# Contrast adjustment on one core: scaling and clip moved from ScalarE and VectorE to two whole-tile VectorE passes

## The chip, the cores and the metric

The kernel runs on one core of one Trainium2 chip. The metric is the device time of one execution in microseconds (us). The timed figure is longer than the span of the same execution in its profile (239.35 against 237.5 for the kernel before), so timed and traced numbers are kept apart below.

## The reference

```python
def reference(x, factor):                      # x: 16 x 3 x 512 x 512 float32, factor 1.5
    mean = np.mean(x, axis=(2, 3), keepdims=True)
    return np.clip(mean + factor * (x - mean), 0, 1).astype(np.float32)
```

The input is read once and an output of the same size is written once: 50.33 MB each way. An image must be summed before its first pixel can be written, so the work is load, sum, scale and clip, store.

## The kernel before

The 48 images are 12 tiles of 128 x 8192 float32 (4.19 MB each). A ring of six tile buffers lies in on-chip memory. SyncE issues the loads, ScalarE issues the stores. A tile is summed by two engines side by side (VectorE 4352 columns, ScalarE 3840), a matmul with a constant block matrix adds up the partitions of each image, and the result is a per-partition bias. Then ScalarE computes `relu(1.5 * x + bias)` in place, in two chunks, and VectorE takes the minimum with 1 behind it.

```python
BUFS = 6
CHUNKS = (5120, 3072)
SHORT = 2048
FIRST = (SHORT, 3072, 3072)
SUM = 4352
# ... (cut: pools, blockw, load)
    def compute(t):
        xt = ring[:, t % BUFS, :]
        sums = rpool.tile([P, 2], f32, name="sums")
        nc.vector.tensor_reduce(                                            # L78
            out=sums[:, 0:1], in_=xt[:, 0:SUM], axis=mybir.AxisListType.X, op=Alu.add
        )
        junk = jpool.tile([P, ROW - SUM], f32, name="junk")
        nc.scalar.activation(                                               # L82
            out=junk, in_=xt[:, SUM:ROW], func=Act.Copy, accum_out=sums[:, 1:2]
        )
        pbias = psum.tile([P, 1], f32, name="pbias")
        nc.tensor.matmul(pbias, blockw, sums[:, 1:2], start=True, stop=False)   # L86
        nc.tensor.matmul(pbias, blockw, sums[:, 0:1], start=False, stop=True)   # L87
        bias = bpool.tile([P, 1], f32, name="bias")
        nc.vector.tensor_copy(out=bias, in_=pbias)                          # L89
        c = 0
        for n in FIRST if t == 0 else CHUNKS:
            part = xt[:, c : c + n]
            nc.scalar.activation(out=part, in_=part, func=Act.Relu, bias=bias, scale=factor)  # L93
            nc.vector.tensor_scalar(out=part, in0=part, scalar1=1.0, scalar2=None, op0=Alu.min)  # L94
            # ... (cut: tile 0 stores its first 2048 columns early)
            c += n
        store(t, FIRST[0] if t == 0 else 0, ROW)                            # issued by ScalarE, L101
# ...
        load(0, c1=SHORT); load(0, c0=SHORT); load(1); load(2, n=2); load(4, n=2)
        for t in range(n_tiles):
            compute(t)
            if t + BUFS < n_tiles:
                load(t + BUFS)             # waits until the store of tile t has landed
```

## Time and profile before

| | kernel before |
|---|---|
| timed, median of the first 3 runs | 239.18 us (239.09 to 239.86) |
| span in the profile | 237.5 us |
| moved | 100.67 MB |
| VectorE busy, ScalarE busy | 111.9 us (47%), 131.1 us (55%) |
| rate from 100 to 200 us | 435 GB/s |

The page of the kernel before: busy time by engine, then the rows of VectorE, ScalarE and DMA over 40 equal slices of the span (a digit is tenths of the slice busy), the rate of each slice, and the chain of waits that ended last.

```profile
PE 14.0 (6%) x48; PEld 12.0 (5%) x48; DVE 111.9 (47%) x49; ACT 131.1 (55%) x50; POOL 0.9 (0%) x9
...
DVE  0073846161964343782928739173462733716000
ACT  2058678056679046769676796753680690593000
...
DMA  7999999999999999999999999999999999999996
GB/s 297 410 441 441 417 441 356 459 430 451 436 419 430 403 436 441 441 441 436 441 436 436 425 419 414 436 443 441 436 441 430 441 436 419 425 414 441 441 441 265
...
DMA 57%; DVE 19%; ACT 10%; another core or an unknown queue 3%; issue 1%; PE 1%; SPq 1%; ACTq 0%
```

Read the DMA row first: it is at 9 from the second slice to the last but one, while both compute engines have holes throughout. A single slice's rate scatters, so the rate is better read from a longer stretch. The view by stretches gives, for each, its length, the busy time of each engine, the clock, the DMA share and the rate:

```profile
100.00:200.00 100.00, 7.03 (x24) 6.00 (x24) 56.71 (x25) 64.82 (x24) 0.00 (x0) 1.00 1.01 435
```

The groups of instructions by shape give what one piece of work costs. After the count come total busy time, mean nanoseconds of one, and the engine's idle time before them.

```profile
L78 DVE TENSOR_REDUCE sums<-ring 128x1 f32<-128x4352 f32 x12 | 56.2, 4682 | 41.4 <-DMA ring<-in_x_dram 41.4
L93 ACT ACTIVATE ring<-ring,bias 128x5120 f32<-128x5120 f32 x11 | 50.2, 4562 | 19.9 <-DVE bias L89 11.0 <-issue 8.9
...
L94 DVE TENSOR_SCALAR ring<-ring 128x5120 f32<-128x5120 f32 x11 | 31.1, 2827 | 51.5 <-ACT ring L93 51.5
```

VectorE waits 41.4 us in total for loads: compute waits for data. The timeline shows the last tile, from its load's landing (202.79, the reduce's start) to its store's issue (217.53). The columns are start, duration, engine and instruction.

```profile
202.79 4.69 DVE L78 TENSOR_REDUCE sums<-ring 128x1 f32<-128x4352 f32 x1 [4.65 <-DMA ring<-in_x_dram]
...
208.16 0.16 DVE L89 COPY bias<-pbias 128x1 f32<-128x1 f32 x1 [0.68 <-PE pbias L87]
208.40 7.31 ACT L93 ACTIVATE ring<-ring,bias 128x5120 f32<-128x5120 f32 x2 [2.05 <-issue]
212.99 4.51 DVE L94 TENSOR_SCALAR ring<-ring 128x5120 f32<-128x5120 f32 x2 [4.68 <-ACT ring L93]
217.53 0.34 ACTq L101 DMA_DIRECT2D out_dram<-ring  x1
```

The chain of this tile is 217.53 - 202.79 = 14.74 us. The store lands at the span's end, 20 us after its issue.

### The profile page before, as it was taken

The numbers are of one execution on the slowest core, as the hardware profiler recorded it, in microseconds if no ns is written. First come the engines' busy times: TensorE is split into PE (matmuls) and PEld (weight loads), VectorE is DVE, ScalarE is ACT, GpSimd is POOL, SyncE is SP. The second block draws the span as 40 slices with busy tenths as digits, with TensorE's granted clock in tenths as the row PEclk, the third lists the DMA queues.
The fourth block names the chain that finished last, engine by engine and source line by source line (L and its number), as shares of the span: only waits on it lengthen the run. The fifth ranks groups of instructions, "written<-read, shape, count | busy, mean of one in ns | idle before, by whom it ended". The sixth has DMA issues, their size and how long they took to land.

```text
span 237.5 us, 307 instructions
## 1 busy us (share of the span) xinstructions
PE 14.0 (6%) x48; PEld 12.0 (5%) x48; DVE 111.9 (47%) x49; ACT 131.1 (55%) x50; POOL 0.9 (0%) x9
## 2 busy tenths in 40 slices
PE   0010010001010001010010100100100100100000
PEld 0010010001010001010010100100100100100000
DVE  0073846161964343782928739173462733716000
ACT  2058678056679046769676796753680690593000
POOL 1000000000000000000000000000000000000000
DMA  7999999999999999999999999999999999999996
GB/s 297 410 441 441 417 441 356 459 430 451 436 419 430 403 436 441 441 441 436 441 436 436 425 419 414 436 443 441 436 441 430 441 436 419 425 414 441 441 441 265
DMA packets 3713, 100.67 MB, mean 424 GB/s; under 512 B 384, under 2 KB 384, under 8 KB 384
## 3 DMA queue, kind: packets, MB, share of 16 engines
q1 hardware_dynamic: 1840, 50.33, 49.7%
q10 hardware_dynamic: 1872, 50.33, 49.1%
q14 instruction: 1, 0.01, 0.0%
HBM read 50.33 MB, written 50.33 MB: 424 GB/s over the span
## 4 chain that ended last, share of the span: by engine, by line
DMA 57%; DVE 19%; ACT 10%; another core or an unknown queue 3%; issue 1%; PE 1%; SPq 1%; ACTq 0%
DMA ring<-in_x_dram 40%; DMA out_dram<-ring 17%; ACT ring L93 10%; DVE ring L94 9%; DVE sums L78 9%; PE pbias L87 1%; SPq L73 1%; DVE bias L89 0%; ACTq L93 0%
## 5 line engine op out<-in xcount | busy, mean ns | idle before, releaser
L93 ACT ACTIVATE ring<-ring,bias 128x3072 f32<-128x3072 f32 (+2 forms) x25 | 87.9, 3564 | 22.1 <-DVE bias L89 13.2
L94 DVE TENSOR_SCALAR ring<-ring 128x3072 f32<-128x3072 f32 (+2 forms) x25 | 54.3, 2208 | 56.1 <-ACT ring L93 56.1
L78 DVE TENSOR_REDUCE sums<-ring 128x1 f32<-128x4352 f32 x12 | 56.2, 4682 | 41.4 <-DMA ring<-in_x_dram 41.4
L82 ACT ACTIVATE junk<-ring 128x3840 f32<-128x3840 f32 x12 | 40.8, 3402 | 61.8 <-DMA ring<-in_x_dram 48.5
L86 PE MATMUL pbias<-sums,blockw 128*128 128x1 f32 x24 | 7.0, 361 | 190.1 <-ACT junk L82 190.1
L86 PEld LDWEIGHTS pbias<-sums,blockw 128*128 128x128 f32 x24 | 6.0, 311 | 191.0 <-ACT junk L82 174.6
L87 PE MATMUL pbias<-sums,blockw 128*128 128x1 f32 x24 | 7.0, 362 | 3.9 <-DVE sums L78 3.4
L87 PEld LDWEIGHTS pbias<-sums,blockw 128*128 128x128 f32 x24 | 6.0, 311 | 5.0 <-DVE sums L78 5.0
L89 DVE COPY bias<-pbias 128x1 f32<-128x1 f32 x12 | 1.9, 158 | 8.1 <-PE pbias L87 8.1
L82 ACT ACTIVATION_READ_ACCUMULATOR junk<-ring 128x1 f32 x12 | 2.2, 186 | 0.0
L82 ACT ACT_TABLE_LOAD x1 | 1.3, 1283 | 0.7 <-PEq L129 0.7
L60 POOL MEMSET blockw<- 32x32 f32 x4 | 0.5, 117 | 0.2
L58 POOL MEMSET blockw<- 128x128 f32 x1 | 0.2, 205 | 0.3 <-POOLq L129 0.3
L129 POOL MEMSET const-bfloat16-1.0<- 128x1 bf16 x1 | 0.1, 112 | 0.0
L129 POOL MEMSET const-uint8-127<- 128x1 uint8 x1 | 0.1, 112 | 0.0
L129 POOL MEMSET const-float32-1.0<- 128x1 f32 x1 | 0.1, 109 | 0.0
L129 POOL MEMSET const-float32-0.0<- 128x1 f32 x1 | 0.1, 104 | 0.2 <-issue 0.2
## 6 DMA issues: line engine op xcount, KB each, us to landing
out_dram<-ring ACTq DMA_DIRECT2D x11, 4096.0 KB, 37.9
ring<-in_x_dram SPq DMA_DIRECT2D x7, 4096.0 KB, 47.1
ring<-in_x_dram SPq DMA_DIRECT2D x2, 8192.0 KB, 65.5
ring<-in_x_dram SPq DMA_DIRECT2D x1, 3072.0 KB, 11.6
out_dram<-ring ACTq DMA_DIRECT2D x1, 3072.0 KB, 29.6
ring<-in_x_dram SPq DMA_DIRECT2D x1, 1024.0 KB, 4.8
out_dram<-ring ACTq DMA_DIRECT2D x1, 1024.0 KB, 18.7
```

The source lines that it names most:

```text
L58: nc.gpsimd.memset(blockw, 0.0)
L60: nc.gpsimd.memset(blockw[a : a + ppi, a : a + ppi], wconst)
L73: nc.sync.dma_start(out=ring[:, b : b + n, c0:c1], in_=src)
L78: nc.vector.tensor_reduce(out=sums[:, 0:1], in_=xt[:, 0:SUM], axis=mybir.AxisListType.X, op=Alu.add)
L82: nc.scalar.activation(out=junk, in_=xt[:, SUM:ROW], func=Act.Copy, accum_out=sums[:, 1:2])
L86: nc.tensor.matmul(pbias, blockw, sums[:, 1:2], start=True, stop=False)
L87: nc.tensor.matmul(pbias, blockw, sums[:, 0:1], start=False, stop=True)
L89: nc.vector.tensor_copy(out=bias, in_=pbias)
L93: nc.scalar.activation(out=part, in_=part, func=Act.Relu, bias=bias, scale=factor)
L94: nc.vector.tensor_scalar(out=part, in0=part, scalar1=1.0, scalar2=None, op0=Alu.min)
L129: nc = _bacc.Bacc("TRN2", target_bir_lowering=False, num_devices=1)
```

## The change

The intent: take the scaling off ScalarE (25 Relu passes, 87.9 us), which is slower per column here than VectorE, and let VectorE do it as two passes over a whole tile (tile 0 in two pieces): first `1.5 * x + bias`, then maximum with 0 and minimum with 1. ScalarE keeps its share of the sums and issues the stores. One matmul with two columns replaces two accumulating ones, and a two-column reduce adds them while it leaves PSUM, the memory that matmuls write to. Small results get a column per tile instead of a pool of two buffers. Loads, stores and the ring stay.

```diff
-CHUNKS = (5120, 3072)
-FIRST = (SHORT, 3072, 3072)
+FIRST = (SHORT, ROW - SHORT)
 ... (cut: pools; sums, bias, pbias become tiles with a column or two per tile)
-        nc.tensor.matmul(pbias, blockw, sums[:, 1:2], start=True, stop=False)
-        nc.tensor.matmul(pbias, blockw, sums[:, 0:1], start=False, stop=True)
-        bias = bpool.tile([P, 1], f32, name="bias")
-        nc.vector.tensor_copy(out=bias, in_=pbias)
+        pair = pbias[:, 2 * t : 2 * t + 2]
+        nc.tensor.matmul(pair, blockw, own, start=True, stop=True)
+        shift = bias[:, t : t + 1]
+        nc.vector.tensor_reduce(out=shift, in_=pair, axis=mybir.AxisListType.X, op=Alu.add)
         c = 0
-        for n in FIRST if t == 0 else CHUNKS:
+        for n in FIRST if t == 0 else [ROW]:
             part = xt[:, c : c + n]
-            nc.scalar.activation(out=part, in_=part, func=Act.Relu, bias=bias, scale=factor)
-            nc.vector.tensor_scalar(out=part, in0=part, scalar1=1.0, scalar2=None, op0=Alu.min)
-            if t == 0 and c == FIRST[0]:
-                store(t, 0, c)
+            nc.vector.tensor_scalar(
+                out=part, in0=part, scalar1=factor, scalar2=shift, op0=Alu.mult, op1=Alu.add
+            )
+            nc.vector.tensor_scalar(
+                out=part, in0=part, scalar1=0.0, scalar2=1.0, op0=Alu.max, op1=Alu.min
+            )
+            store(t, c, c + n)
             c += n
-        store(t, FIRST[0] if t == 0 else 0, ROW)
```

More of the change, by code (lines that the diff above doesn't have):

```diff
@@ L51 @@
     xpool = ctx.enter_context(tc.tile_pool(name="xpool", bufs=1))
-    jpool = ctx.enter_context(tc.tile_pool(name="jpool", bufs=1))
-    rpool = ctx.enter_context(tc.tile_pool(name="rpool", bufs=2))
-    bpool = ctx.enter_context(tc.tile_pool(name="bpool", bufs=2))
-    psum = ctx.enter_context(tc.tile_pool(name="psum", bufs=2, space=bass.MemoryType.PSUM))
+    small = ctx.enter_context(tc.tile_pool(name="small", bufs=1))
+    psum = ctx.enter_context(tc.tile_pool(name="psum", bufs=1, space=bass.MemoryType.PSUM))
+    sums = small.tile([P, 2 * n_tiles], f32, name="sums")
+    bias = small.tile([P, n_tiles], f32, name="bias")
+    junk = small.tile([P, ROW - SUM], f32, name="junk")
+    pbias = psum.tile([P, 2 * n_tiles], f32, name="pbias")
     blockw = consts.tile([P, P], f32, name="blockw")
@@ L76, in compute @@
         xt = ring[:, t % BUFS, :]
-        sums = rpool.tile([P, 2], f32, name="sums")
+        own = sums[:, 2 * t : 2 * t + 2]
         nc.vector.tensor_reduce(
-            out=sums[:, 0:1], in_=xt[:, 0:SUM], axis=mybir.AxisListType.X, op=Alu.add
+            out=own[:, 0:1], in_=xt[:, 0:SUM], axis=mybir.AxisListType.X, op=Alu.add
         )
-        junk = jpool.tile([P, ROW - SUM], f32, name="junk")
-        nc.scalar.activation(
-            out=junk, in_=xt[:, SUM:ROW], func=Act.Copy, accum_out=sums[:, 1:2]
-        )
-        pbias = psum.tile([P, 1], f32, name="pbias")
-        nc.tensor.matmul(pbias, blockw, sums[:, 1:2], start=True, stop=False)
-        nc.tensor.matmul(pbias, blockw, sums[:, 0:1], start=False, stop=True)
-        bias = bpool.tile([P, 1], f32, name="bias")
-        nc.vector.tensor_copy(out=bias, in_=pbias)
+        nc.scalar.activation(out=junk, in_=xt[:, SUM:ROW], func=Act.Copy, accum_out=own[:, 1:2])
+        pair = pbias[:, 2 * t : 2 * t + 2]
+        nc.tensor.matmul(pair, blockw, own, start=True, stop=True)
+        shift = bias[:, t : t + 1]
+        nc.vector.tensor_reduce(out=shift, in_=pair, axis=mybir.AxisListType.X, op=Alu.add)
         c = 0
-        for n in FIRST if t == 0 else CHUNKS:
+        for n in FIRST if t == 0 else [ROW]:
             part = xt[:, c : c + n]
-            nc.scalar.activation(out=part, in_=part, func=Act.Relu, bias=bias, scale=factor)
-            nc.vector.tensor_scalar(out=part, in0=part, scalar1=1.0, scalar2=None, op0=Alu.min)
-            if t == 0 and c == FIRST[0]:
-                store(t, 0, c)
+            nc.vector.tensor_scalar(
[5 more added lines that the diff above has]
+            store(t, c, c + n)
             c += n
-        store(t, FIRST[0] if t == 0 else 0, ROW)
     def store(t, c0, c1):
```

## The prediction

> What bounds the kernel now. It moves 100.67 MB. The page's slices show the DMA row at 9 or more in slices 2 to 39, and the stretch 100 to 200 us moved 435 GB/s. The Trainium skill (DMA: Bandwidth & Descriptors, "Where 436 GB/s comes from") puts the fabric ceiling at 435.2 GB/s; this trace agrees in its steady part. 100.67 MB at 435 GB/s is 231.4 us (estimate); with 2.1 us until the first load moves and some ramp and receipt, that is nearly the whole span of 237.5 us. VectorE is busy 47%, ScalarE 55%: neither limits. The chain of waits is 57% DMA, and its compute pieces run under other tiles' transfers. The last load landed at 202.8, the last store was issued at 217.5 and landed about 20 us later, although its 4 MB alone need only about 10: it still queued behind the store before it. So compute latency is hidden even at the end.
>
> What the change removes, adds and moves (groups by shape):
> - ScalarE loses 25 Relu passes, 87.9 us. It keeps 40.8 us of sums: busy about 44 us (19%).
> - VectorE loses 54.3 us of min passes and gains two passes per tile. The min passes took 1.226, 1.760 and 2.827 us for 2048, 3072 and 5120 columns: 0.160 us + 0.521 ns per column. A pass over 8192 columns is then 4.43 us (estimate), two are 8.85 us. VectorE is busy about 165 us (69%): 56 reduce, about 107 passes, 2 for biases. This takes the pass with the per-partition bias to be as fast as the pass with constants: the Trainium skill (DVE: scalar operands, raw-bit mode, write accounting and state across instructions, "Scalar operands") says that such a scalar does not take up the second tensor stream. No run here shows it yet.
> - PE: 24 matmul calls become 12. Bias: a 2-column reduce in place of a copy, about 0.17 us both.
> - Stores, loads, their sizes, queues and the ring of 6 are the same.
>
> Critical path of a tile, load landed to store issued. Before: reduce 4.69, PE 0.6, bias 0.17, Relu of 5120 4.57, last two min 4.51, with gaps 14.7 us. After: 4.69 + 0.6 + 0.17 + 2 x 4.43 and gaps = about 14.5 us. ScalarE's sum of the next tile (3.6) still runs beside VectorE's 4.69 us reduce. A tile needs 19.3 us of DMA (8.39 MB at 435 GB/s, estimate), so 14.5 us fits with about 5 to spare. First store at about 21 us (21.8 before), last one at about 217.
>
> So nearly nothing lies on the critical path: 87.9 us of ScalarE work saved buys no time. Predicted 239.0 us, range 238.1 to 240.2. Faster by over 2%: 0.01; within 2%: 0.95; slower by over 2%: 0.04.
>
> What would show it: DMA row still 9 from slice 2 to 39, about 435 GB/s in mid-span; both clip passes near 4.43 us; VectorE near 69%, ScalarE near 19%; VectorE waiting only for loads and the short PE step; store issued about 14.5 us after its load landed.
>
> What would make it wrong: the biased pass running at one column per cycle, about 8.7 us. The tile then takes about 18.8 us, VectorE becomes the limit, and 12.9 + 12 x 18.8 + a last store of about 10 us gives about 248 us (slower). Or the DMA rate depending on how loads and stores mix, if store times shift. A gain over 2% is hardly possible: the DMA engines have only about 5 us to spare.

## The result, and the profile after

| | before | after |
|---|---|---|
| timed, median of 6 runs each | 239.2 us | 239.5 us (239.47 to 239.55) |
| ratio after to before | | 1.0009, 95% interval 0.9996 to 1.0022 |
| span in the profile | 237.5 us | 237.6 us |
| VectorE busy | 111.9 us (47%) | 164.8 us (69%) |
| ScalarE busy | 131.1 us (55%) | 43.2 us (18%) |

Here and below a ratio is the mean time of one kernel's runs over the mean of the other's runs in the same rounds, so it is not quite the ratio of the medians quoted beside it. Executions over 1.5% slower than the fastest of the same kernel are left out of the means. Nearly 88 us of ScalarE work disappeared and 53 us of VectorE work appeared, and nothing measurable happened to the time.

The same parts of the page of the changed kernel:

```profile
PE 6.7 (3%) x24; PEld 6.0 (3%) x24; DVE 164.8 (69%) x50; ACT 43.2 (18%) x25; POOL 0.9 (0%) x9
...
DVE  0079989168989258989989899874892892895000
ACT  2050230050140040050500505004101300500000
...
DMA  7999998999999989999999999999999999999996
GB/s 301 406 441 441 419 441 357 459 441 441 441 441 430 436 381 430 441 441 441 441 441 441 441 430 403 408 436 441 441 441 441 441 441 441 430 399 408 441 441 265
...
DMA 56%; DVE 29%; another core or an unknown queue 3%; PE 1%; issue 1%; SPq 1%; DVEq 0%
```

The VectorE row filled up, the ScalarE row emptied, and the DMA row is as it was, apart from two slices that read 8. The mid-span stretch of the changed kernel, to be laid beside that of before:

```profile
100.00:200.00 100.00, 3.36 (x12) 3.01 (x12) 82.89 (x25) 20.98 (x12) 0.00 (x0) 1.00 1.01 435
```

The third busy figure (VectorE) rose from 56.71 to 82.89 and the fourth (ScalarE) fell from 64.82 to 20.98; the last figure, the rate, is 435 in both. The groups by shape of the changed kernel:

```profile
L82 DVE TENSOR_REDUCE sums<-ring 128x1 f32<-128x4352 f32 x12 | 56.2, 4682 | 41.5 <-DMA ring<-in_x_dram 41.5
L93 DVE TENSOR_SCALAR ring<-ring,bias 128x8192 f32<-128x8192 f32 x11 | 49.3, 4486 | 1.5 <-DVE bias L89 0.5
L96 DVE TENSOR_SCALAR ring<-ring 128x8192 f32<-128x8192 f32 x11 | 48.7, 4427 | 0.4
```

VectorE's wait for loads is 41.5 us against 41.4: compute still waits for data, by the same amount. The last tile of the changed kernel:

```profile
202.25 4.68 DVE L82 TENSOR_REDUCE sums<-ring 128x1 f32<-128x4352 f32 x1 [4.74 <-DMA ring<-in_x_dram]
...
207.67 0.16 DVE L89 TENSOR_REDUCE bias<-pbias 128x1 f32<-128x2 f32 x1 [0.74 <-PE pbias L87]
208.33 4.49 DVE L93 TENSOR_SCALAR ring<-ring,bias 128x8192 f32<-128x8192 f32 x1 [0.50 <-DVE bias L89]
212.85 4.43 DVE L96 TENSOR_SCALAR ring<-ring 128x8192 f32<-128x8192 f32 x1
217.31 0.34 ACTq L103 DMA_DIRECT2D out_dram<-ring  x1
```

Its chain is 217.31 - 202.25 = 15.06 us, of which 0.5 us is an idle gap before the biased pass that the tile before it did not have (there, 14.66 us). Its store again lands 20 us later, at the span's end.

### The profile page after: what moved, and what is told of

The parts are those of the page before. It is cut to its first block, busy times and chain, and to the rows that moved or that the text cites. A ratio compares the mean times of both kernels' runs of the same rounds, so it can differ in the third digit from the quotient of the medians.

```text
span 237.6 us, 245 instructions
## 1 busy us (share of the span) xinstructions
PE 6.7 (3%) x24; PEld 6.0 (3%) x24; DVE 164.8 (69%) x50; ACT 43.2 (18%) x25; POOL 0.9 (0%) x9
## 4 chain that ended last, share of the span: by engine, by line
DMA 56%; DVE 29%; another core or an unknown queue 3%; PE 1%; issue 1%; SPq 1%; DVEq 0%
DMA ring<-in_x_dram 40%; DMA out_dram<-ring 16%; DVE sums L82 10%; DVE ring L93 9%; DVE ring L96 9%; PE pbias L87 1%; SPq L77 1%; DVE bias L89 0%; DVEq L93 0%
## 5 line engine op out<-in xcount | busy, mean ns | idle before, releaser
L82 DVE TENSOR_REDUCE sums<-ring 128x1 f32<-128x4352 f32 x12 | 56.2, 4682 | 41.5 <-DMA ring<-in_x_dram 41.5
L93 DVE TENSOR_SCALAR ring<-ring,bias 128x8192 f32<-128x8192 f32 (+2 forms) x13 | 54.0, 4157 | 1.6 <-DVE bias L89 0.5
L96 DVE TENSOR_SCALAR ring<-ring 128x8192 f32<-128x8192 f32 (+2 forms) x13 | 53.3, 4099 | 0.5
L87 PE MATMUL pbias<-sums,blockw 128*128 128x2 f32 x24 | 6.7, 349 | 200.9 <-DVE sums L82 200.9
L87 PEld LDWEIGHTS pbias<-sums,blockw 128*128 128x128 f32 x24 | 6.0, 312 | 201.5 <-issue 117.0
L89 DVE TENSOR_REDUCE bias<-pbias 128x1 f32<-128x2 f32 x12 | 1.9, 160 | 8.9 <-PE pbias L87 8.9
```

Source lines behind the costliest of these rows:

```text
L82: nc.vector.tensor_reduce(out=own[:, 0:1], in_=xt[:, 0:SUM], axis=mybir.AxisListType.X, op=Alu.add)
L87: nc.tensor.matmul(pair, blockw, own, start=True, stop=True)
L89: nc.vector.tensor_reduce(out=shift, in_=pair, axis=mybir.AxisListType.X, op=Alu.add)
L93: nc.vector.tensor_scalar(out=part, in0=part, scalar1=factor, scalar2=shift, op0=Alu.mult, op1=Alu.add)
L96: nc.vector.tensor_scalar(out=part, in0=part, scalar1=0.0, scalar2=1.0, op0=Alu.max, op1=Alu.min)
```

## The experiments

Two readings fit this result. **A**: the DMA engines set the time, and compute is hidden behind the transfers of other tiles. **B**: the chain of a tile, near 14.7 us in both kernels, sets the time, and the change merely reproduced it. A third, **C**: the change saved time, but a busier VectorE slowed the transfers by as much. All kernels below are edits of the changed kernel, unless said otherwise. Those called wrong serve for timing only. The others were correct.

### No compute at all

```diff
-        (sums, matmul, bias and both passes of every tile)
             store(t, c, c + n)
```

> All compute is taken out of the changed kernel; each tile is stored as soon as it has landed (wrong result on purpose). Theory A (the DMA engines set the time, compute latency is hidden behind other tiles' transfers): 238 to 239.5 us, within 1% of the kernel before, DMA row still 9 in the slices. Rival B (the 14.6 us latency chain of a tile, which both kernels share by coincidence, sets the time): clearly faster, by tens of us. Rival C (the change did save time, but busier VectorE slows the transfers by as much): with no engine touching the on-chip memory the rate in mid-span rises above 435 GB/s and the time falls below 236.

Measured: 238.99 us against 239.32 for the kernel before, ratio 0.9984 (0.9969 to 0.9999), span 237.3 us. The mid-span stretch of this kernel, where the only engine with a column left is GpSimd:

```profile
100.00:200.00 100.00, 0.00 (x0) 1.00 1.01 435
```

Its DMA row, as A expected:

```profile
DMA  7999999999999999999999999999999999999996
```

The kernel without compute is 0.16% faster than the kernel before (0.01 to 0.31% by the interval). So about 0.2% is what both versions can still gain without moving fewer bytes or moving them differently. B falls: with no chain at all, the time stays. C falls too: with no engine touching on-chip memory the rate is 435 GB/s, as with VectorE 83% busy. This agrees with the Trainium skill (SBUF — State Buffer, "SBUF: two separate sides"), which says that engine and DMA accesses use separate ports and do not contend.

### More VectorE work: half a pass, and a whole pass

```diff
             nc.vector.tensor_scalar(
                 out=part, in0=part, scalar1=0.0, scalar2=1.0, op0=Alu.max, op1=Alu.min
             )
+            again = part[:, : n // 2]          # extra_half; the whole of part in extra_full
+            nc.vector.tensor_scalar(
+                out=again, in0=again, scalar1=0.0, scalar2=1.0, op0=Alu.max, op1=Alu.min
+            )
```

> The changed kernel with a third clip pass over half of each piece, which changes no result: 0.16 + 4096 x 0.521 ns = 2.3 us more per tile, chain of a tile about 16.9 us. A: 12.8 until the first tile is in, 12 x 16.9, and about 12 for the last store give about 228, under the 237.6 us that DMA needs: same time, within 0.5%. B: 12 x 2.3 = 27 us slower, about 267.

> The changed kernel with a third clip pass over the whole of each piece, which changes no result: 4.43 us more per tile, chain of a tile about 19.0 us. A: 12.8 + 12 x 19.0 + about 10 to 12 for the last store, which now queues behind nothing, = 251 to 253 us in the trace: slower by 5 to 7%, with VectorE busy over 85% and idle time in the DMA row near the end, although 19.0 is under the 19.3 us of DMA per tile of my prediction. B: 12 x 4.43 = 53 us slower, about 293.

Measured, half a pass: 239.78 us, ratio 1.0016 (1.0001 to 1.0031); as A had it. From the page of this kernel, busy time and the chain of waits; from its view of waits, what VectorE waited for:

```profile
PE 6.7 (3%) x24; PEld 6.0 (3%) x24; DVE 192.3 (81%) x63; ACT 43.2 (18%) x25; POOL 0.9 (0%) x9
...
DVE 67%; DMA 20%; PE 2%; issue 1%; another core or an unknown queue 1%; SPq 1%; DVEq 0%
```

```profile
DVE sums L82 <- DMA ring<-in_x_dram: 18.3, 3, 12.9
```

VectorE got 192.3 - 164.8 = 27.5 us more work. Its wait for loads shrank from 41.5 to 18.3 us, which took up 23.2; the last store was issued at 221.97 instead of 217.31, which took up 4.7, and that store landed 16 us after issue instead of 20. The span grew by 0.3 us. Note the chain: it now names VectorE for 67%, although a kernel without VectorE is hardly faster. The chain goes back from the last event through one releaser each time, and one long run of back-to-back VectorE work is a valid path; it does not tell that another path, the full DMA queues, was as long.

Measured, a whole pass: 255.70 us, ratio 1.0681 (1.0663 to 1.0699), span 253.9 us, VectorE busy 86%; A's range of 251 to 253 missed by 1 us and B's 293 far off. The rows of the page of this kernel:

```profile
DVE  0089989989989989989989989989989989989910
...
DMA  7999999999999999999999999999999999077077
GB/s 289 454 413 428 454 439 372 413 454 413 485 423 413 413 480 423 418 413 475 428 413 413 475 434 413 413 470 434 418 413 456 444 418 418 5 330 330 0 330 330
```

```profile
241.99 0.34 ACTq L106 DMA_DIRECT2D out_dram<-ring  x1
```

Now the DMA row has holes: the loads are finished, and the last two stores come one by one, 19.0 us apart (the one before was issued at 222.99), each alone in the queues. The last one, with nothing queued ahead, took 253.9 - 241.99 = 11.9 us. So 16 us were lost although a period of 19.0 us is below the 19.3 us that a tile's traffic needs at 435 GB/s. The reason is at the two ends. The first tile's load and extra pieces put about 14.0 us in front (241.99 - 12 x 19.0), and 11.9 us come behind. To end by 237.6 the last store has to leave by 225.7, so the longest period that hides is (225.7 - 14.0) / 12 = 17.6 us (an estimate from these traces, which takes the last store to run alone). It lies between the 16.9 us that cost nothing and the 19.0 us that did.

### Fewer stored bytes: the two kernels without the DMA limit

```diff
-            store(t, c, c + n)
             c += n
+        store(t, 0, SHORT)                  # quarter pair; in the lastq pair: store(t, ROW - SHORT, ROW)
```

The same edit was made to the kernel before (its early store of tile 0 went too). These are wrong: three quarters of the output stay unwritten.

> The kernel before, storing only 2048 of 8192 columns of each tile after the tile's last pass (wrong result on purpose: the rest is not written). 62.9 MB need about 145 us at 435 GB/s, so the DMA limit is lifted. A: now the chain of a tile sets the pace: 12.9 + 12 x 14.65 + about 4 for the last small store = about 193 us in the trace, about 194.5 timed; VectorE idle only for its short waits. If the time stayed near 239, neither DMA nor this chain would be the limit and A would fall.

> The changed kernel, storing only 2048 of 8192 columns of each tile, as in quarter_before (wrong result on purpose). A and the claim of equal latency: 12.8 + 12 x 14.57 + about 4 = about 192 us in the trace, about 193.5 timed, at most 1% faster than quarter_before, VectorE busy over 85%. If the change had a real gain or loss that DMA hid, it would show here as a difference of more than 2% between the two.

Measured: kernel before with quarter stores 196.28 us, changed kernel with quarter stores 196.73 us; ratios to the full kernel before 0.8202 and 0.8220. With the DMA limit lifted the chain does set the pace, as A expected, 1.8 and 3.2 us above the estimates. In both, VectorE still waited for one more load after the first tile's, about 2 us; from then on it waited for none, and the last store took 4.7 to 4.8 us where about 4 was assumed. But the changed kernel came out 0.2% slower where I had expected it slightly faster. The traces show that the pair was uneven: in the kernel before, the first 2048 columns are finished by the first of the two min passes, so the store left before the tile was done. The last tile's passes and its store in that run:

```profile
186.62 4.51 DVE L94 TENSOR_SCALAR ring<-ring 128x5120 f32<-128x5120 f32 x2 [4.69 <-ACT ring L93]
189.48 0.34 ACTq L99 DMA_DIRECT2D out_dram<-ring  x1
```

The store leaves at 189.48 while the passes end at 191.13. So I repeated the pair with the last 2048 columns.

> The kernel before, storing only the last 2048 columns of each tile (wrong result on purpose). quarter_before stored the first 2048, which the first min pass (5120 columns) finishes, so its stores left 1.7 us before the tile was done and that pair was not even. Here the store waits for the tile's last pass. A: last store issued at about 191.2 us in place of 189.5, so about 198.0 us timed, 1.7 us more than quarter_before.

> The changed kernel, storing only the last 2048 columns of each tile (wrong result on purpose): the even partner of lastq_before. The period of a tile is 14.54 against 14.62 us in the quarter pair, 12 tiles, so 1 us less: A: about 196.7 us timed as in quarter_after, 0.4 to 0.8% faster than lastq_before. A hidden gain or loss of the change would show as more than 2%.

Measured: 197.65 us and 196.95 us, ratios to the full kernel before 0.8248 and 0.8220; one over the other, the changed kernel is 0.34% faster, just under the range I gave. The last two stores of the kernel before, and then of the changed kernel:

```profile
176.51 0.34 ACTq L99 DMA_DIRECT2D out_dram<-ring  x1
...
191.13 0.34 ACTq L99 DMA_DIRECT2D out_dram<-ring  x1
```

```profile
175.62 0.34 ACTq L103 DMA_DIRECT2D out_dram<-ring  x1
...
190.16 0.34 ACTq L103 DMA_DIRECT2D out_dram<-ring  x1
```

A tile takes 14.62 us before and 14.54 us after. So the change has no hidden gain of any size: even where compute sets the time, two serial VectorE passes are worth the pipelined ScalarE and VectorE pair to within 0.08 us per tile.

### The small results in pools of two again

```diff
-        own = sums[:, 2 * t : 2 * t + 2]
+        own = rpool.tile([P, 2], f32, name="sums")          # rpool: bufs=2
 ... (bias, pbias and junk likewise; made to the quarter-store kernel)
```

> quarter_after with small results in pools of two buffers again (the third part of the change undone; the two passes and single matmul stay). A: reuse waits held nothing up; within 0.5% of quarter_after, chain per tile within 0.1 us. If a column per tile had freed something, this would be slower by over 1%, with waits on the sums or the bias.

Measured: 196.65 us against 196.73, ratios 0.8217 and 0.8220; the last store leaves at 190.03 against 190.02. A column per tile buys nothing measurable, even where the chain sets the time. Wrong, as the kernel it was made from.

### The last tile in four pieces

```diff
-        for n in FIRST if t == 0 else [ROW]:
+        for n in FIRST if t == 0 else LAST if t == n_tiles - 1 else [ROW]:   # LAST = (2048,) * 4
```

> The changed kernel with the last tile clipped and stored in four pieces of 2048 columns, so that its first store is issued about 6.6 us earlier. A: the DMA engines are busy with the store before it anyway, so an earlier store buys at most the raggedness of the last few us: 0 to 0.8 us faster (0 to 0.3%). If the last tile's compute latency were exposed, it would be about 6 us faster.

Measured: 239.60 us, ratio 1.0011 (0.9998 to 1.0025), no different from the changed kernel's 1.0009. The first store of the last tile was issued at 210.90 instead of 217.31 and gained nothing, so the last tile's latency is not exposed. The small gain that I allowed for did not show either.

### Fewer ring buffers

```diff
-BUFS = 6
+BUFS = 3                                   # ring4: BUFS = 4; the first loads cut to match
```

> The changed kernel with a ring of 3 buffers in place of 6. A: the latency is hidden only because other tiles' loads and stores are queued meanwhile; with 3 buffers of which one is being computed on for 14.5 us, the queues run dry at times: 2 to 6% slower (about 245 to 250), holes in the DMA row, VectorE waiting for loads. If B held and DMA had much to spare, 3 buffers would suffice and the time would stay within 1%.

> The changed kernel with a ring of 4 buffers. A: with 3 buffers the time rose by 5.7%; a tile holds a buffer for at least 9.6 us of load, 14.5 of compute and 9.6 of store, and with one more buffer there is nearly always a load and a store queued: within 1% of the kernel before. If any buffer taken away costs in proportion, it would be 3 to 4% slower.

Measured with 3 buffers: 253.72 us (251.57 to 255.61), ratio 1.0569 (1.0511 to 1.0627). The 5.7% lies inside the 2 to 6% expected, the microseconds above the 245 to 250 written beside it. Its four runs scatter by 1.6%, and the profiled one was the slowest, so I take only the direction from its trace: VectorE's wait for loads is longer (65.6 us against 41.5). The holes I expected in the DMA row are not there before the last few slices. There, in this slow run, the last store left at 241.74 and ran alone for 12.1 us; over 100 to 200 us the rate was 424 GB/s instead of 435, and why was not settled. With 4 buffers: 241.16 us, ratio 1.0065 (1.0044 to 1.0086), within the 1% expected. What VectorE waited for with 4 buffers:

```profile
DVE sums L82 <- DMA ring<-in_x_dram: 51.3, 9, 13.0
```

Its DMA row, and its last store:

```profile
DMA  7999999999999999999999999999999999999696
```

```profile
227.36 0.34 ACTq L103 DMA_DIRECT2D out_dram<-ring  x1
```

Its rate over 100 to 200 us is still 435 GB/s. The loss is at the end: the last tile's reduce starts at 212.29 instead of 202.25, its store leaves 10 us later than with six buffers, and that store runs alone for 12.0 us.

The latency is hidden because loads of other tiles are queued ahead: six buffers hide nearly all of it, four lose 0.65% at the end, three do not suffice.

No correct version here beats the kernel before. The run without compute says why: whatever is done on the engines, about 0.2% is to be had while the transfers stay as they are.

## Why the prediction was right

- **What bounds the kernel.** Right. The predicted time was 239.0 us, the measured one 239.5. Rate and DMA row behaved as said, but for two slices at 8 instead of 9. The 435 GB/s agree with the ceiling that the Trainium skill works out (DMA: Bandwidth & Descriptors, "Where 436 GB/s comes from"), with loads and stores mixed. The same section also says that the HBM side, at about 358 GB/s, binds such transfers; with one core running, this trace does not agree. What holds the rate at 435, the DMA engines, the fabric or HBM, no run here separates. The experiment without compute shows the bound directly; the prediction had only argued it.
- **Cost of the passes.** Right. Predicted 4.43 us for both; measured 4.427 for the pass with constants and 4.486 for the one with the per-partition bias. So the bias does not halve the rate, as the Trainium skill's statement suggested (DVE: scalar operands, raw-bit mode, write accounting and state across instructions, "Scalar operands"), but the biased pass takes 0.05 to 0.06 us more per instruction, which the sum left out. The two passes also differ in their operations, so that this is the price of the bias operand is not shown. VectorE 164.8 us against about 165, ScalarE 43.2 against about 44.
- **Latency of a tile.** Right in kind, slightly low: predicted about 14.5 us from landing to store, measured 14.66 for a usual tile and 15.06 for the last one. The missing pieces are the 0.06 us of the biased pass and the small gaps: the matmul with its hand-overs took 0.74 us between reduce and bias (0.68 before), where the prediction had 0.6 and left the gaps unsized. The 0.5 us gap before the last tile's biased pass is not explained. It cost nothing, as the run with the last tile in four pieces shows: a store issued 6.4 us earlier gained nothing either.
- **"14.5 us fits with about 5 to spare."** Mis-sized. The prediction compared the chain with the 19.3 us of DMA per tile, as if the pipeline had no ends. (In its own case for being wrong it did count both ends and came to 248 us for a tile of 18.8, so its two statements did not agree.) A tile of 19.0 us, within that budget, cost 6.8%; one of 16.9 us cost nothing. With the first tile's arrival and the last store counted, about 17.6 us hide (an estimate, above), so about 3 us were to spare. This also makes the "about 10 us" for a lone last store too small: it took 11.9.
- **"87.9 us of ScalarE work saved buys no time."** Right, and now shown. The Trainium skill (ScalarE: Activation LUTs, "Rules for kernel authors") says to use VectorE rather than ScalarE for relu, min, add and multiply. The trace agrees on the instruction: 4.562 us against 2.827 for 5120 columns, though the Relu pass also scales and adds. But one ScalarE pass became one more VectorE pass, and neither engine was the limit.

## What to carry to other kernels

Before you optimise an engine, find the floor of the transfers alone: take the compute out and time what is left. If that is within a fraction of a per cent, only fewer bytes or other transfers can help, and a large shift of busy time between engines will show as nothing. When you ask how much more compute would hide, do not compare rates per tile alone: add the time before the first tile can start and the time of the last store with nothing around it, and keep enough buffers that loads are always queued.

## What the Trainium skill lacked or had wrong

- VectorE: DVE Perf Modes, and DVE: scalar operands, raw-bit mode, write accounting and state across instructions: neither gives the cost of a per-partition scalar in a VectorE instruction. Here a pass with one took 51 to 60 ns more than the pass with constants, whatever its length: 1.286 against 1.226 us at 2048 columns, 3.411 against 3.360 at 6144, 4.486 against 4.427 at 8192. The operations differ too, so the scalar's own share is not separated.
- DMA: Bandwidth & Descriptors has its rate table for loads alone. Here loads and stores mixed half and half moved 435 GB/s over 100 us, with compute running and without.
- Perfetto Trace Analysis names the buffer count as a possible cause of consistent bubbles, but not how to size a ring against the latency to be hidden. Here six buffers hid it to within about 0.2%, four cost 0.65%, three 5.7%.
- No page that I read warns that a chain of waits can name an engine that is not the limit: with half a pass added, VectorE made up 67% of the chain, in a kernel whose transfers alone took 99.7% as long (237.3 of 237.9 us).
